# Layer boundary of a two-layer decoder trunk: a residual ahead of the next weights' splits, and norm weights applied per K tile

## The chip, the cores and the metric

The kernel runs on one core of a Trainium2 chip. The metric is the device time of one execution in microseconds (us); smaller is better. The engines of the core work in parallel, each through its own list of instructions in order: PE (matrix products and transposes), ACT (activations, copies), DVE (vector work), POOL (vector work as well) and SP, which here only issues the transfers from memory. An instruction starts when the one ahead of it on its engine has gone and the semaphores that it waits for are set.

## The reference

Two layers over 256 positions of width 1024, each x ← x + RMSNorm_post(mixer(RMSNorm_pre(x))). Layer 0 mixes with gated linear attention, layer 1 with compressed, selected and sliding-window attention. What matters here is the step from one layer to the next:

```
def rms_norm(x, g):
    xf = x.astype(jnp.float32)
    y = xf * lax.rsqrt(jnp.mean(xf * xf, axis=-1, keepdims=True) + NORM_EPS)
    return (y * g.astype(jnp.float32)).astype(x.dtype)
...
    for i in range(DEPTH):
        h = rms_norm(x, pre_norm[i])
        ...
            y = gla_mixer(h, ..., gla_w_out[j])      # ends in o @ w_out
        ...
            y = nsa_mixer(h, positions, nsa_w_in[j], ...)   # begins with h @ w_in
        x = x + rms_norm(y.astype(x.dtype), post_norm[i])
```

## The kernel before

The 256 positions are two tiles of 128 rows (t = 0, 1). The width of 1024 is 8 K tiles of 128, k0 to k7. To keep float32 accuracy in the faster product format, each operand is split into a rounded half, hi, and a remainder, lo = value − hi; a product of one K tile is then three matmuls, hi·hi, lo·hi and hi·lo (`mm3`). ACT writes every hi, DVE or POOL every lo.

**Weights** come in chunks of up to 512 columns. A chunk is 4 loads of two K tiles each into `raw` buffers, and 8 splits (`split_unit`): ACT copies a K tile of `raw` to `hi`, and DVE or POOL (by the table `LOS`) subtracts. Around the boundary these are `ch_o` (layer 0's output weights), `ch_kc` and `ch_ks` (the first two chunks of layer 1's input weights) and `ch_kw` after them.

**The boundary** is the loop over t that begins with `out_proj` (line 775). `out_proj(t)` multiplies layer 0's result with `ch_o` into two PSUM banks of 512 columns and calls `residual`: for each half, ACT squares the bank and sums the squares, DVE scales the bank by the norm weights into `yg`; after the second half POOL takes the power −0.5 of the sum, and DVE adds both halves to `X`. `pre_T(t, c)` then transposes `X[:, t]` on PE, four K tiles into one PSUM bank (c = 0: k0 to k3, c = 1: k4 to k7), applies layer 1's pre-norm weights (`gT`, one per row of the transpose) and splits the result into `hT`, the operand of every product of layer 1. `rms(t)` computes tile t's own factor, which is applied later.

Behind the boundary PE computes `kc_part(0)` and `ks_part(0)` (24 matmuls each, of tile 0 with `ch_kc` and `ch_ks`), then `kc_part(1)`, `ks_part(1)`, and then the products with `ch_kw`. In this text kc(0) is the 24 matmuls of `kc_part(0)`, and so on. They take k0 to k7 in turn. Small transposes stand between them: that of `vecs` (line 846; its copy on DVE is line 847) and the 16 of line 853.

The order on each engine is made when the program is built: a scheduler places the instructions by its own estimate of the time, within the order of the code and the extra edges of `after(...)`. Before, one such edge holds the first split of `ch_ks` behind the last hi of tile 0's `hT` (`ks_after`). The line numbers below are those of the kernel before; in the kernel after they differ by up to two.

Of the kernel before, what the change touches and what calls it, by code (L numbers as in the profile page):

```python
# [9 lines left out]
F32 = mybir.dt.float32  # L10
F32R = mybir.dt.float32r
I32 = mybir.dt.int32
AF = mybir.ActivationFunctionType
ALU = mybir.AluOpType
AX = mybir.AxisListType

P = 128
# [3 lines left out]
KT = D // P  # L21
# [66 lines left out]
def hybrid_kernel(ctx: ExitStack, tc: tile.TileContext, x, positions, pre_norm, post_norm,  # L88
# [3 lines left out]
    nc = tc.nc  # L92
    base = ctx.enter_context(tc.tile_pool(name="base", bufs=1))
# [4 lines left out]
    def nm(s):  # L98
        _n[0] += 1
        return f"{s}_{_n[0]}"  # L100

    def bank(tag="t"):
        return ps.tile([P, 512], F32, tag=tag, name=nm(tag), bufs=BANKS[tag])

    def f(ap):
        return ap.bitcast(F32)

    def after(ins, prev):

        if prev is not None:  # L110
            tc.add_manual_dep(ins.ins, prev.ins.name, mybir.DependencyInfo(
                mybir.DependencyClass.NoSync, mybir.DependencyReason.DATA), reason="issue order")
        return ins
# [103 lines left out]
    def chain(first, final):  # L217

        after(first, last[0])
        last[0] = final  # L220

    def proj(chunk, hT, t, tag="acc"):

        o = bank(tag)
        for k in range(KT):
            a, b = mm3(o[:, :chunk.n], [h[:, k, t * P:(t + 1) * P] for h in hT], chunk.part(k), k == 0, k == KT - 1)
            first = a if k == 0 else first
            chunk.mm[t * KT + k] = a
        chain(first, b)
        return o  # L230
# [24 lines left out]
    def rstd_of(ss, n, m, by=1.0):  # L255
# [4 lines left out]
        nc.gpsimd.tensor_tensor(r[:, :m], v[:, :m], half[:, :m], op=ALU.pow)  # L260
        return r

    def residual(t, o, gb):

        ss = base.tile([P, 8], F32, tag="ss", name=nm("ss"), bufs=4)
        yg = [base.tile([P, H], F32, tag="xg", name=nm("yg"), bufs=2) for _ in range(2)]

        def done(n):
            nc.scalar.activation(yg[n], o[n], AF.Square, accum_out=ss[:, n:n + 1])  # L269
            if n == 0:  # L270
                nc.vector.tensor_scalar(ss[:, 2:3], ss[:, 0:1], D * EPS, None, op0=ALU.add)
            else:

                nc.vector.tensor_add(ss[:, 4:5], ss[:, 1:2], ss[:, 2:3])
                nc.gpsimd.tensor_tensor(ss[:, 3:4], ss[:, 4:5], half[:, :1], op=ALU.pow)
            nc.vector.scalar_tensor_tensor(yg[n], o[n], float(D ** 0.5), gb[:, n * H:(n + 1) * H], op0=ALU.mult,  # L276
                                           op1=ALU.mult)
            if n == 1:
                for m in range(2):
                    xx = X[:, t, m * H:(m + 1) * H]  # L280
                    nc.vector.scalar_tensor_tensor(xx, yg[m], ss[:, 3:4], xx, op0=ALU.mult, op1=ALU.add)
        return done
# [8 lines left out]
    def new_hT():  # L291
        return [base.tile([P, KT, S], F32R, tag=f"hT{n}", name=nm("hT")) for n in "hl"]
# [2 lines left out]
        nc.scalar.activation(hi, bv, AF.Copy)  # L295
        nc.vector.tensor_sub(lo, bv, f(hi))

    def pre_T(t, c, layer, hT, tag, prev=None):

        b = bank(tag)  # L300
        for k in range(4):
            m = nc.tensor.transpose(b[:, k * P:(k + 1) * P], X[:, t, (c * 4 + k) * P:(c * 4 + k + 1) * P], ident)
            if layer == t == 0:
                chain(m, m)
        xg = base.tile([P, 4, P], F32, tag="xg", name=nm("xg"), bufs=2)
        g = gT[:, layer * KT + c * 4:layer * KT + c * 4 + 4]
        nc.vector.tensor_tensor(xg, b.rearrange("p (k n) -> p k n", k=4), g.unsqueeze(2).to_broadcast([P, 4, P]),
                                op=ALU.mult)
        hi, lo = (a[:, c * 4:c * 4 + 4, t * P:(t + 1) * P] for a in hT)
        m = after(nc.scalar.activation(hi, xg, AF.Copy), prev)  # L310
        nc.vector.tensor_sub(lo, xg, f(hi))  # L311
        return m

    onesr = base.tile([P, P], F32R, tag="onesr", name="onesr")
# [3 lines left out]
    def rms(t, prev=None):  # L318

        ss = base.tile([P, 8], F32, tag="ss", name=nm("ss"), bufs=4)  # L320
        for n in range(2):
            jk = base.tile([P, H], F32, tag="of", name=nm("junk"))
            m = after(nc.scalar.activation(jk, X[:, t, n * H:(n + 1) * H], AF.Square, accum_out=ss[:, n:n + 1]), prev)
        nc.vector.tensor_add(ss[:, 2:3], ss[:, 0:1], ss[:, 1:2])
        rs = rstd_of(ss[:, 2:3], D, 1)
        return rs[:, 0:1], m
# [13 lines left out]
    def out_proj(t, chunks, oT, gb):  # L340

        o = [bank("s"), bank("acc" if t else "s")]
        steps = [(k, n) for k in range(4) for n in range(2)] + [(k, n) for n in range(2) for k in range(4, KT)]
        done = residual(t, o, gb)
        for k, n in steps:
            a, b = mm3(o[n], [h[:, k, :] for h in oT[t]], chunks[n].part(k), k == 0, k == KT - 1)
            first = a if k == n == 0 else first
            if k == KT - 1:
                done(n)
        chain(first, b)  # L350
# [42 lines left out]
    hT = new_hT()  # L393
# [92 lines left out]
    gT = base.tile([P, 2 * KT], F32, tag="gT", name="gT")  # L486
# [75 lines left out]
    w, n = wraw[:RANK + 1], RANK + 1  # L562
# [24 lines left out]
    b = bank()  # L587
# [42 lines left out]
    scale = float(np.float32(GDK ** -0.5))  # L630
    aTs, qees, kdds = [], [], []
    for t in range(NT):
# [3 lines left out]
        for hp in range(2):  # L636
            b = bank()
# [4 lines left out]
            bv = b.rearrange("p (h n) -> p h n", h=2)  # L642
            nc.scalar.activation(E[:, 2 * hp:2 * hp + 2, :w], bv[:, :, :w], AF.Exp)
            last_exp = nc.scalar.activation(En[:, 2 * hp:2 * hp + 2, :], bv[:, :, :P], AF.Exp, scale=-1.0)
        if t == 0:
            b = bank()
# [9 lines left out]
        bv = qT[:, :, t * P:(t + 1) * P]  # L656
        nc.vector.scalar_tensor_tensor(qe, bv, scale, E[:, :, :P], op0=ALU.mult, op1=ALU.mult)
        if t == 1:
# [3 lines left out]
                                           op0=ALU.mult, op1=ALU.mult)  # L662
            qee = halves(qee, ("qeeh", "qeel"))
        b = bank()
        for h in range(GH):
            nc.tensor.transpose(b[:, h * P:(h + 1) * P], ksb[:, t, h * P:(h + 1) * P], ident)
        bv = b.rearrange("p (h n) -> p h n", h=GH)
# [26 lines left out]
    for t in range(NT):  # L694
        aT = aTs[t]
        ob = []
        for hp in range(2):
            b = bank("s")
            for hh in range(2):
                h = 2 * hp + hh  # L700
                o = b[:, hh * 256:(hh + 1) * 256]
# [4 lines left out]
        if t == 0:  # L706
            Ssb = [lp.tile([P, GH, GDV], F32R, tag=a, name=nm("S")) for a in ("q", "k")]
            for hp in range(2):
                b = bank("s")
# [8 lines left out]
        for h in range(GH):  # L718
            nc.vector.scalar_tensor_tensor(on[:, h * 256:(h + 1) * 256], ov[h], rs[:, h:h + 1], hn,
                                           op0=ALU.mult, op1=ALU.mult)  # L720
# [6 lines left out]
    for c in range(2):  # L727
# [4 lines left out]
        for t in range(NT):  # L732
            b = bank()
# [36 lines left out]
    hT = new_hT()  # L770
# [3 lines left out]
    for t in range(NT):  # L774
        out_proj(t, ch_o, oT, gpost)
        for c in range(2):
            last_hi = pre_T(t, c, 1, hT, "t")
        if t == 0:
            ks_after = last_hi
        rs1.append(rms(t)[0])  # L780
        for tab in (CSt, SNt):
            nc.vector.tensor_scalar(tab[:, t], tab[:, t], rs1[t], None, op0=ALU.mult)
# [3 lines left out]
    lp = ctx.enter_context(tc.tile_pool(name="l2", bufs=1))  # L786
    ch_kc.split()
    ch_ks = Chunk(w_in, N_KS, 512).load()
    ch_ks.split_unit(ks_after)
    ch_ks.split()  # L790
    vs_sb = lp.tile([P, NT, 256], F32, tag="vs", name="vs_sb")
    vw_sb = lp.tile([P, NT, 256], F32, tag="vw", name="vw_sb")
# [119 lines left out]
    for t in range(NT):  # L912
        o = proj(ch_kw[0], hT, t)
# [4 lines left out]
    for t in range(NT):  # L918
        o = proj(ch_kw[1], hT, t)
        nc.scalar.activation(vw_sb[:, t, 24:], o[:, :232], AF.Copy, scale=rs1[t])  # L920

        g = gates[:, t].rearrange("p h b -> p (h b)")
# [226 lines left out]
    def out_steps(t, before=None):  # L1149

        o = [bank("acc") for _ in range(2)]
        steps = [(k, n) for k in range(6) for n in range(2)] + [(k, n) for n in range(2) for k in range(6, KT)]
        done = residual(t, o, gpost)
        for k, n in steps:
            a, b = mm3(o[n], [h[:, k, :] for h in ofT[t]], ch_o[n].part(k), k == 0, k == KT - 1)
            if before and (k, n) == (LATE, 0):
                after(a, before())
            chain(a, b)
            if k == KT - 1:
                done(n)  # L1160
            yield 1
        for n in range(2):
            sl = slice(n * H, n * H + H)
            dma(out[0, t * P:(t + 1) * P, sl], X[:, t, sl])
# [7 lines left out]
    b = bank()  # L1172
# [8 lines left out]
    b = bank()  # L1181
# [84 lines left out]
```

## Time and profile before

| | before |
|---|---|
| median of 3 runs (lowest, highest) | 298.65 us (298.47, 299.83) |
| the profiled execution | 298.99 us, of which the traced span is 297.1 us |
| PE busy | 283.8 us, 96% of the span |
| DVE, ACT, POOL busy | 213.8, 178.7, 163.8 us |
| mean granted clock of PE | 0.995 |

PE is busy nearly throughout, so the time follows the few places at which it waits. The 1.9 us between the span and the time of the execution lie outside the trace. Times in rows are counted from the start of the span.

### The profile page before, as it was taken

The page shows a single profiled execution, that of the slowest core. Times are in us where ns is not written, and L with a number is a line of the kernel's source. Part 1 is how long each engine was busy: PE and PEld are TensorE (multiplying, and loading weights), DVE is VectorE, ACT ScalarE, POOL GpSimd, SP SyncE. Part 2 cuts the span into 40 slices and gives each one's busy share as a digit, 9 for nine tenths or more (in the row PEclk, how much of TensorE's full clock was granted, in tenths as well). Part 3 has the DMA queues.
Part 4 walks back from the last instruction along what each step waited for, and adds up shares of the span by engine and source line. Part 5 has one row for each costly group of instructions (what it writes and reads, how often), then busy time and mean ns, then how long its engine had stood idle before and what let it go on. Part 6 is the DMA issues. An engine that isn't in the chain of part 4 may idle for free.

```text
span 297.1 us, 5455 instructions
## 1 busy us (share of the span) xinstructions
PE 283.8 (96%) x1836; PEld 238.2 (80%) x1836; DVE 213.8 (72%) x552; ACT 178.7 (60%) x464; POOL 163.8 (55%) x184
## 2 busy tenths in 40 slices
PE   8999999999999999889999999999999979999991
PEld 7788999999999887668897789976887657677560
DVE  1679668854989968577459578799569988686423
ACT  3896788676665665444436526494568896475311
POOL 1396968985376132824539295479596545333200
PEclk9999999999999999999999999999999999999997
DMA  7996488114667244189896575607162000010001
GB/s 205 399 398 207 145 253 273 48 67 146 210 207 221 76 139 141 29 227 348 263 381 185 149 216 165 183 12 225 49 200 86 1 0 2 0 72 2 0 0 71
DMA packets 28300, 44.56 MB, mean 150 GB/s; under 512 B 2865, under 2 KB 12513, under 8 KB 28274
## 3 DMA queue, kind: packets, MB, share of 16 engines
q1 hardware_dynamic: 28242, 44.23, 47.2%
q8 instruction: 14, 0.23, 0.3%
q14 instruction: 12, 0.10, 0.1%
q10 hardware_dynamic: 32, 0.01, 0.0%
HBM read 43.18 MB, written 1.05 MB: 149 GB/s over the span
## 4 chain that ended last, share of the span: by engine, by line
PE 71%; DVE 11%; issue 8%; POOL 4%; ACT 2%; DMA 2%; SPq 0%; POOLq 0%; DVEq 0%; ACTq 0%
PE acc L213 12%; PE acc L211 12%; PE acc L212 12%; PE s L211 4%; PE s L212 4%; PE s L213 4%; PE s L468 4%; PE o L1105 3%; PE t L1091 3%; PE s L1018 3%; PE o L904 2%; DVE lo L196 2%; DVE P L1023 2%; DMA raw<-in_gla_w_in_dram 2%; PE o L1129 1%
## 5 line engine op out<-in xcount | busy, mean ns | idle before, releaser
L196 POOL TENSOR_TENSOR lo<-raw,hi 128x512 fp32r<-128x512 f32 (+2 forms) x63 | 83.6, 1349 | 42.1 <-ACT hi L190 41.1
L190 ACT ACTIVATE hi<-raw 128x512 fp32r<-128x512 f32 (+2 forms) x120 | 62.7, 582 | 17.8 <-DMA raw<-in_nsa_w_in_dram 6.2
L196 DVE TENSOR_TENSOR lo<-raw,hi 128x512 fp32r<-128x512 f32 (+2 forms) x57 | 54.5, 978 | 8.8 <-ACT hi L190 8.6
L1062 POOL TENSOR_SCALAR P<-P,cf 128x128 f32<-128x128 f32 (+1 forms) x64 | 28.0, 456 | 31.9 <-DVE cf L1058 9.1
L211 PE MATMUL acc<-hT,hi 128*128 128x256 f32 x160 | 45.0, 282 | 0.0
L212 PE MATMUL acc<-hT,hi 128*128 128x256 f32 x160 | 44.9, 281 | 0.0
L213 PE MATMUL acc<-hT,lo 128*128 128x256 f32 x160 | 44.5, 281 | 0.0
L1025 ACT ACTIVATE P<-P,mn 128x128 f32<-128x128 f32 (+1 forms) x64 | 28.4, 446 | 14.4 <-DVE mn L1023 10.4
L213 PE MATMUL acc<-hi,hT 128*128 128x512 f32 (+2 forms) x104 | 35.9, 346 | 0.8 <-DVE hT L311 0.8
L211 PE MATMUL acc<-hi,hT 128*128 128x512 f32 (+2 forms) x104 | 35.8, 345 | 0.8 <-DVE yg L276 0.8
L212 PE MATMUL acc<-lo,hT 128*128 128x512 f32 (+2 forms) x104 | 35.4, 341 | 0.0
L212 PEld LDWEIGHTS acc<-hT,hi 128*128 128x128 f32 x160 | 30.1, 188 | 0.3
L211 PEld LDWEIGHTS acc<-hT,hi 128*128 128x128 f32 x160 | 30.1, 188 | 0.1
L213 PEld LDWEIGHTS acc<-hT,lo 128*128 128x128 f32 x160 | 29.8, 188 | 0.0
L1023 DVE CUSTOM_DVE_ANT_0 P<-s,c 128x128 f32<-128x128 f32 (+1 forms) x64 | 20.9, 349 | 6.2 <-PE s L1018 4.8
L211 PEld LDWEIGHTS acc<-hi,hT 128*128 128x128 f32 x104 | 19.6, 188 | 3.7 <-ACT yg L269 1.2
L213 PEld LDWEIGHTS acc<-hi,hT 128*128 128x128 f32 x104 | 19.6, 188 | 3.4 <-DVE hT L311 1.7
L212 PEld LDWEIGHTS acc<-lo,hT 128*128 128x128 f32 x104 | 19.6, 188 | 1.7
L1091 PE MATMUL t<-c,P 128*128 128x128 f32 x96 | 18.3, 286 | 0.3 <-POOL P L1062 0.3
L440 POOL TENSOR_TENSOR lo<-raw,hi 128x512 fp32r<-128x512 f32 (+1 forms) x9 | 12.3, 1390 | 10.2 <-ACT hi L436 10.1
L1018 PE MATMUL s<-kTh,qS 128*128 128x272 f32 (+1 forms) x48 | 15.2, 329 | 2.2 <-DVE mn L1023 1.6
L1091 PEld LDWEIGHTS t<-c,P 128*128 128x128 f32 x96 | 10.9, 140 | 6.7 <-issue 3.5
(270 smaller groups left out, 673.8 us busy)
## 6 DMA issues: line engine op xcount, KB each, us to landing
raw<-in_nsa_w_in_dram SPq DMA_DIRECT2D x24, 512.0 KB, 4.3
raw<-in_gla_w_in_dram SPq DMA_DIRECT2D x12, 512.0 KB, 5.3
raw<-in_gla_w_out_dram SPq DMA_DIRECT2D x8, 512.0 KB, 4.3
raw<-in_nsa_w_out_dram SPq DMA_DIRECT2D x8, 512.0 KB, 4.1
raw<-in_nsa_w_in_dram SPq DMA_DIRECT2D x8, 280.0 KB, 6.1
raw<-in_gla_w_in_dram SPq DMA_DIRECT2D x6, 344.0 KB, 3.1
home<-in_gla_w_in_dram SPq DMA_DIRECT2D x4, 512.0 KB, 6.8
w<-in_nsa_ck_w_dram SPq DMA_DIRECT2D x4, 512.0 KB, 7.4
```

The lines of the kernel that those rows point to most:

```text
L190: m = after(nc.scalar.activation(hi[:, j, :n], raw[:, j, :n], AF.Copy), prev)
L196: eng.tensor_sub(lo[:, j, :n], raw[:, j, :n], f(hi[:, j, :n]))
L211: m = nc.tensor.matmul(o, a[0], b[0], start=start, stop=False, **kw)
L212: nc.tensor.matmul(o, a[0], b[1], start=False, stop=False, **kw)
L213: return m, nc.tensor.matmul(o, a[1], b[0], start=False, stop=stop, **kw)
L440: line(e, eng.tensor_sub(lo[:, j, :n], raw[:, j, :n], f(hi[:, j, :n])))
L468: m = nc.tensor.matmul(o[t][:, :chunk.n], hT[i][:, k, t * P:(t + 1) * P], w[j], start=(k == b == 0), stop=(k == KT - 1 and b == 2))
L1018: pe(nc.tensor.matmul(o, q[i], k[:, g, c0:c1], start=(m == 0), stop=(m == 1)))
L1023: nc.vector.tensor_tensor_reduce(out=o, in0=src, in1=masks[br], op0=ALU.add, op1=ALU.min, scale=-0.125, scalar=3.0e38, accum_out=self.mn[: ...
L1025: nc.scalar.activation(o, o, AF.Exp, scale=-1.0, bias=self.mn[:, j:j + 1], accum_out=self.sm[:, j:j + 1])
L1062: nc.gpsimd.tensor_scalar(o, o, cf[:, i * 2 + br:i * 2 + br + 1], 1.0, op0=ALU.mult, op1=ALU.mult)
L1091: pe(nc.tensor.transpose(b[:, i * P:(i + 1) * P], self.Pt[i][:, c0:c0 + P], ident))
```

## The change

Three edits. In `pre_T` the product with the norm weights, the copy to hi and the subtraction, each over four K tiles at once and through a buffer `xg`, become one pair per K tile straight from the PSUM bank: ACT copies with the weight as its scale, DVE multiplies and subtracts in one instruction. The buffer `xg`, which the residual's `yg` shares, is no longer used there. The edge on the first split of `ch_ks` now starts at the last square of tile 1's residual instead of at tile 0's hi.

```
-    def pre_T(t, c, layer, hT, tag, prev=None):
+    def pre_T(t, c, layer, hT, tag):
...
-        xg = base.tile([P, 4, P], F32, tag="xg", name=nm("xg"), bufs=2)
-        g = gT[:, layer * KT + c * 4:layer * KT + c * 4 + 4]
-        nc.vector.tensor_tensor(xg, b.rearrange("p (k n) -> p k n", k=4), g.unsqueeze(2).to_broadcast([P, 4, P]),
-                                op=ALU.mult)
-        hi, lo = (a[:, c * 4:c * 4 + 4, t * P:(t + 1) * P] for a in hT)
-        m = after(nc.scalar.activation(hi, xg, AF.Copy), prev)
-        nc.vector.tensor_sub(lo, xg, f(hi))
+        for k in range(4):
+            i = c * 4 + k
+            hi, lo = (a[:, i, t * P:(t + 1) * P] for a in hT)
+            bv, g = b[:, k * P:(k + 1) * P], gT[:, layer * KT + i:layer * KT + i + 1]
+            m = nc.scalar.activation(hi, bv, AF.Copy, scale=g)
+            nc.vector.scalar_tensor_tensor(lo, bv, g, f(hi), op0=ALU.mult, op1=ALU.subtract)
         return m
...
-            nc.scalar.activation(yg[n], o[n], AF.Square, accum_out=ss[:, n:n + 1])
+            squared[0] = nc.scalar.activation(yg[n], o[n], AF.Square, accum_out=ss[:, n:n + 1])
...
-            last_hi = pre_T(t, c, 1, hT, "t")
-        if t == 0:
-            ks_after = last_hi
+            pre_T(t, c, 1, hT, "t")
...
-    ch_ks.split_unit(ks_after)
+    ch_ks.split_unit(squared[0])
```

What this makes of the order. On ACT at the boundary, from the last square of `rms(0)` on, the order before was (`xg_237` and `xg_239` hold k0 to k3 and k4 to k7 of tile 0; `hi_271` to `hi_277` are the four pairs of `ch_ks`; `yg_248` and `yg_249` the two squares of tile 1's residual):

```order
L323 ACTIVATE junk_242_1410,ss_240_1407<-x_sb_73 128x512
L310 ACTIVATE hT_225_1317<-xg_237_1394 128x4x128
L310 ACTIVATE hT_225_1317<-xg_239_1403 128x4x128
L190 ACTIVATE hi_271_1547<-raw_267_1539 128x512 x2
L190 ACTIVATE hi_273_1553<-raw_268_1541 128x512 x2
L190 ACTIVATE hi_275_1559<-raw_269_1543 128x512 x2
L190 ACTIVATE hi_277_1565<-raw_270_1545 128x512 x2
L269 ACTIVATE yg_248_1422,ss_247_1421<-s_245_1419 128x512
L269 ACTIVATE yg_249_1423,ss_247_1421<-acc_246_1420 128x512
```

Now it is as follows, from the second square on (bank `t_236` holds k0 to k3 of tile 0, `t_237` k4 to k7; the square of the first half, three pieces of `t_236`, k0 to k2, and two of `t_237`, k4 and k5, stand ahead of these rows; `hi_267` to `hi_273` are the pairs of `ch_ks`):

```order
L271 ACTIVATE yg_247_1431,ss_245_1429<-acc_244_1428 128x512
L190 ACTIVATE hi_267_1563<-raw_263_1555 128x512 x2
L190 ACTIVATE hi_269_1569<-raw_264_1557 128x512 x2
L190 ACTIVATE hi_271_1575<-raw_265_1559 128x512
L311 ACTIVATE hT_225_1317<-t_237_1402,gT_126 128x128
L190 ACTIVATE hi_271_1575<-raw_265_1559 128x512
L190 ACTIVATE hi_273_1581<-raw_266_1561 128x512 x2
L311 ACTIVATE hT_225_1317<-t_236_1389,gT_126 128x128
```

The squares moved ahead of the eight splits; the fourth piece of `t_236`, which is k3 of tile 0, now stands behind all eight of them, and the third of `t_237`, k6, among them.

On DVE the order now is, from the third piece of `t_236` (k2) on (`lo_268` and `lo_270` are the DVE's four splits of `ch_ks`; before, they stood behind all of tile 0's `hT` and ahead of the residual):

```order
L312 SCALAR_TENSOR_TENSOR hT_226_1318<-t_236_1389,gT_126,hT_225_1317 128x128
L276 TENSOR_TENSOR ss_245_1429<-ss_245_1429 128x1
L278 SCALAR_TENSOR_TENSOR yg_247_1431<-acc_244_1428,gpost_148_858 128x512
L196 TENSOR_TENSOR lo_268_1564<-raw_263_1555,hi_267_1563 128x512
L283 SCALAR_TENSOR_TENSOR x_sb_73<-yg_246_1430,ss_245_1429,x_sb_73 128x512
L283 SCALAR_TENSOR_TENSOR x_sb_73<-yg_247_1431,ss_245_1429,x_sb_73 128x512
L196 TENSOR_TENSOR lo_268_1564<-raw_263_1555,hi_267_1563 128x512
L196 TENSOR_TENSOR lo_270_1570<-raw_264_1557,hi_269_1569 128x512 x2
L312 SCALAR_TENSOR_TENSOR hT_226_1318<-t_237_1402,gT_126,hT_225_1317 128x128
L847 COPY vT_1610<-o_279_1638 128x32
L312 SCALAR_TENSOR_TENSOR hT_226_1318<-t_236_1389,gT_126,hT_225_1317 128x128
```

The residual of tile 1 moved ahead of three of the four splits, and the lo of k3 (the last row) stands behind all of them and behind the copy of `vecs`.

On PE the rows of kc(0) that use k3 now are these (`acc_277` is its bank; `t_248` is the first bank of tile 1's transposes):

```order
L213 MATMUL acc_277_1611<-hi_257_1537,hT_226_1318 128x512
L846 MATMUL o_279_1638<-c0_64,vecs_1597 128x32
L211 MATMUL acc_277_1611<-hi_257_1537,hT_225_1317 128x512
L212 MATMUL acc_277_1611<-lo_258_1538,hT_225_1317 128x512
L304 MATMUL t_248_1489<-c0_64,x_sb_73 128x128 x4
L213 MATMUL acc_277_1611<-hi_257_1537,hT_226_1318 128x512
```

The transpose of `vecs` and tile 1's transposes moved into kc(0); before, they stood behind ks(0). The other four transposes of tile 1 now stand ahead of the last matmul of kc(0), and the 16 of line 853 behind the sixth matmul of kc(1).

## Rows read from the trace of the kernel before

**Rows 1.** Windows: busy us and count per engine, PE's granted clock, DMA.

```profile
115.90:144.50 28.60, 26.46 (x143) 20.32 (x143) 18.54 (x42) 13.87 (x33) 13.30 (x15) 1.00 0.65 194
144.50:290.90 146.40, 143.57 (x949) 112.71 (x947) 108.92 (x363) 84.60 (x250) 78.96 (x101) 1.00 0.34 106
```

**Rows 2.** Chain that ended last, at the boundary: start, us, engine and line.

```profile
124.73 0.52 POOL ss L275
125.27 1.32 DVE x_sb L281
...
131.84 1.32 DVE hT L311
```

**Rows 3.** Timeline of PE: start, us, line, tiles; in brackets idle and releaser.

```profile
113.66 1.03 PE L302 MATMUL t<-c,x_sb 128*128 128x128 f32 x8
...
115.69 0.40 PE L213 MATMUL acc<-hi,oT 128*128 128x512 f32 x1
116.16 0.50 PE L211 MATMUL acc<-hi,hT 128*128 128x512 f32 x1
...
121.88 0.40 PE L213 MATMUL acc<-hi,hT 128*128 128x512 f32 x1
123.04 0.47 PE L211 MATMUL acc<-hi,hT 128*128 128x512 f32 x1 [0.76 <-DVE yg L276]
...
130.56 0.69 PE L853 MATMUL t<-c,rt 128*64 128x64 f32 x16 [0.49 <-DVE vT L847]
...
131.65 0.50 PE L211 MATMUL acc<-hi,hT 128*128 128x512 f32 x1
...
133.21 0.50 PE L213 MATMUL acc<-hi,hT 128*128 128x512 f32 x1 [0.83 <-DVE hT L311]
...
144.49 0.29 PE L211 MATMUL acc<-hi,hT 128*128 128x280 f32 x1
```

**Rows 4.** Timeline of ACT at the boundary.

```profile
116.61 4.26 ACT L190 ACTIVATE hi<-raw 128x512 fp32r<-128x512 f32 x8
120.77 0.57 ACT L269 ACTIVATE yg<-s 128x512 f32<-128x512 f32 x1
```

**Rows 5.** Timeline of DVE at the boundary.

```profile
110.00 3.49 DVE L196 TENSOR_TENSOR lo<-raw,hi 128x512 fp32r<-128x512 f32 x2
...
114.75 1.28 DVE L307 TENSOR_TENSOR xg<-t,gT 128x512 f32<-128x512 f32 x2
...
117.35 2.49 DVE L196 TENSOR_TENSOR lo<-raw,hi 128x512 fp32r<-128x512 f32 x4
...
122.21 0.68 DVE L276 SCALAR_TENSOR_TENSOR yg<-acc,gpost 128x512 f32<-128x512 f32 x1
```

**Rows 6.** Timeline of POOL at the boundary.

```profile
109.65 3.29 POOL L196 TENSOR_TENSOR lo<-raw,hi 128x512 fp32r<-128x512 f32 x2 [1.02 <-ACT hi L190]
...
119.43 5.29 POOL L196 TENSOR_TENSOR lo<-raw,hi 128x512 fp32r<-128x512 f32 x4 [5.05 <-ACT hi L190]
```

**Rows 7.** Instructions of lines 419 and 424 (layer 0's pieces): ns min/median/max.

```profile
L419 ACT ACTIVATE hT<-t,gT x8: 348/366/378, 5.3 to 8.2; 128x128 fp32r<-128x128 f32 x8
...
L424 DVE SCALAR_TENSOR_TENSOR hT<-t,gT,hT x8: 341/343/351, 6.5 to 9.4; 128x128 fp32r<-128x128 f32 x8
```

**Rows 8.** Instructions that write vecs: SP's issue, and the landing of its transfers.

```profile
L125 SPq DMA_DIRECT2D vecs<-in_nsa_pe_v_dram x1: 418/418/418, 124.9 to 124.9; - x1
...
DMA to landing us min/median/max: 1.7/1.7/1.8
```

**Rows 9.** Timeline of SP: the first transfer behind the boundary.

```profile
122.96 0.88 SPq L125 DMA_DIRECT2D w<-in_nsa_ck_w_dram  x2
```

**Rows 10.** Windows at the end of the span, columns as in rows 1.

```profile
290.50:291.00 0.50, 0.41 (x2) 0.00 (x0) 0.50 (x1) 0.05 (x1) 0.00 (x0) 1.00 0.00 0
...
293.50:294.00 0.50, 0.00 (x0) 0.00 (x0) 0.41 (x1) 0.00 (x0) 0.00 (x0) 1.00 0.00 0
294.00:294.50 0.50, 0.00 (x0) 0.00 (x0) 0.00 (x0) 0.00 (x0) 0.00 (x0) 0.61 0.77 303
```

More of the change, by code (lines that the diff above doesn't have):

```diff
@@ L261, in rstd_of @@
         return r
+    squared = [None]
     def residual(t, o, gb):
```

## The prediction

> **What bounds the kernel now.** The windows on either side of the moment at which PE begins `ch_kw` come first [rows 1]. From 144.5 to 290.9 us PE is busy for 143.57 of 146.40 us: behind the boundary it has 2.83 us of slack in all, so whatever the boundary gains or loses arrives at the end nearly whole. From 115.9 to 144.5 it is idle for 2.14 us, and the change can win only there. PE's timeline names the places [rows 3]: out_proj(1) ends at 115.92 (its last matmul starts at 115.69, and 20 of kc(0)'s gaps up to 121.88 are 0.233 us each), kc(0) begins at 116.16; ks(0) begins at 123.04, where the row says 0.76 idle, because its bank is freed only when DVE has scaled tile 1's residual; line 853 waits 0.49 for the copy of `vecs`; kc(1) begins at 131.65 and waits 0.83 for tile 1's `hT`. The chain of waits gives the reason: between 124.73 and 133.2 it runs off PE, through the power, the update of `X` and the last subtraction into `hT` of tile 1 [rows 2]. That chain starts late because the two squares of the residual (120.77 and 0.57 later) stand behind eight splits that ACT began at 116.61 [rows 4]. So the slot is real, and the waits that the change could remove sum to 0.24 + 0.76 + 0.49 + 0.83 = 2.3 us.
>
> **The change, part by part.** *The squares ahead of the splits.* ACT and DVE do the same residual work, some 4 us earlier. It frees the bank of ks(0) before PE wants it, and starts tile 1's update of `X` sooner. The transfers of layer 1's small tensors move along: the first one waited for the scaling by `gpost`, which ended at 122.21 + 0.68 = 122.89 against the issue at 122.96 [rows 5, 9].
>
> *The pieces per K tile.* Removed for each tile are two products into `xg`, two copies and two subtractions over 512 columns. Added are eight ACT pieces of 0.37 us and eight DVE pieces of 0.34 us, priced by layer 0's same instructions [rows 7]. For two tiles that makes 5.9 us of ACT and 5.5 us of DVE. For tile 1 they lie beside ks(0) and kc(1) on PE, which need nothing from them until kc(1) begins, and I cost them at nothing; without that cover each pair of one bank would cost 0.7 us, since hi and lo of a bank alternate in the built order. For tile 0 they stand on the path: PE takes k0 to k7 in turn and needs hi and lo of each.
>
> *What is late now.* The built order puts the hi of k3 behind all eight splits of `ch_ks` on ACT, and its lo behind three splits on DVE. ACT, DVE and POOL take their lists in order, so this is a wait that no early finish elsewhere can lift. I walk it through.
>
> ACT: the eight transposes of tile 0 begin at 113.66 and take 1.03 [rows 3], so the first bank is there at about 114.2 and hi of k0 at 114.55. DVE comes free where its first `xg` stood, at 114.75 [rows 5]; it now scales the first half first (0.68), so lo of k0 ends at 115.85. Hi and lo alternate with the other bank's pieces in between: hi of k2 ends at 116.95, its lo at 117.3. Then the second square (0.57) to 117.5; eight splits at 0.52 (116.61 to 120.77 for eight [rows 4]) and the piece of k6 among them (0.37) to 122.05; hi of k3 at 122.4.
>
> DVE: the sum of squares is there at 117.6; scaling (0.68), one split (0.62, as 2.49 for four [rows 5]), two updates of `X` (1.32 in the chain [rows 2]) take it to 120.35. Then three splits, and POOL begins its own four at 120.3, when ACT has written their hi. That price is the open one. With POOL idle a DVE split takes 0.62; beside two POOL splits (109.65, 3.29 for two) two DVE splits took 3.49, 1.75 each [rows 5, 6]. The bounds are 0.62 and 1.75; I take 1.75, since here too POOL runs splits without a break from before the first of the three to after the last, 5.29 for four [rows 6]. The three end at 125.65, the piece of k6 and the copy of `vecs` (0.3 together) follow, and lo of k3 ends at 126.3.
>
> The Trainium skill bears on this price: "SBUF — State Buffer", section "Who interferes with whom", says that a DVE instruction with two SBUF inputs and a GpSimd instruction that reads SBUF exclude each other, and that the second to issue waits for the whole of the first. By it each of the three would wait out one POOL split of about 1.3 and then run its own 0.62, some 1.9 instead of 1.75, and the sum below would be 0.5 us more. The page also frees instructions with one SBUF input from this, which would leave the pieces themselves at 0.34.
>
> PE, against that: out_proj(1) ends at 115.92; kc(0) starts there, 0.24 earlier than before, and k0 to k2 are nine matmuls, to 118.02. Then the transpose of `vecs`: its transfers begin when DVE has scaled the second half, at 118.4 instead of 122.89; the last one was issued 1.95 later and landed 1.7 after that [rows 8, 9], so 122.1, and PE stands until then. Next hi of k3: two matmuls from 122.45 to 122.9. Then tile 1's first transposes wait for the bank that lo of k3 frees, and the third matmul of k3 for that lo itself: 126.4. So PE waits 4.4 us and then 3.5 us. From there on nothing waits: four transposes 0.5 (half of 1.03), twelve matmuls 2.8, four transposes 0.5, one matmul 0.2: 130.4. ks(0), 24 matmuls, 5.6: 136.0. kc(1): six matmuls, line 853 (130.56 to 131.65, 1.1), 18 matmuls: 142.7. ks(1) with four transposes of `dup`, 6.1: 148.8. There `ch_kw` begins, which before was 144.49 [rows 3]. Its loads start some 3 us earlier than before, so they don't hold it.
>
> **Sum:** 148.8 − 144.5 = 4.3 us later. As a check, the new waits are 7.9 us; the old ones, 2.3, go, and tile 1's transposes and `vecs`, which then stood alone between two projections, now overlap waits or matmuls. On the profiled execution this makes 298.99 + 4.3 = 303.3 us; the median of the runs shown is 0.34 lower than that execution, so 303.0 us.
>
> **The rivals.** *PE's clock falls in the new waits.* At the end of the span PE's last matmul ended at 290.91, and the granted clock was still 1.00 in the half microsecond up to 294.0 and fell to half (2.4 to 1.2 GHz) in the next one: some 3.2 us without work were enough [rows 10]. The two new waits, 4.4 and 3.5 us, are longer than that, with only two matmuls and one small transpose between them. Against it: those three are work. If the clock falls, matmuls from 126.4 on run at half speed until it returns. No row shows how long that takes; a stretch as long as the fall took (3.2 us) would cost 1.6 us, twice that 3.2: 304.6 to 306.2 us. The Trainium skill, "TensorE: Matmul & The Clock Gate", section "What's actually happening", says that an idle engine is gated to 1.2 GHz and that sustained work brings 2.4 GHz back; the tail agrees with its first half, and no row here shows its second.
>
> *DVE isn't slowed.* If the three splits take 0.62 each, DVE is through at 122.3, lo of k3 follows its hi at 122.9, and the second wait (3.5) is gone: +0.8, 299.5 us. For it speaks that DVE's four at 117.35 took 2.49, against it that POOL was idle then until 119.43 [rows 5, 6].
>
> *The delay is given back later.* All of PE's slack behind the boundary is 2.83 us [rows 1]. Were all of it waits for supplies that now come in time, +1.5 would be left: 300.1 us. Against it: the loads and splits behind the boundary follow the buffers that PE, DVE and POOL free, and so move with them.
>
> *Faster.* The old waits go (2.3, and about 1.3 that transposes and `vecs` cost alone) and PE doesn't stand at k3: 4.3 − 7.9 = −3.6, 295.0 us. It needs hi of k3 when PE has done k2. The point from which it decides is a total of 3.6 us for the new waits: with the second one gone, hi of k3 would have to come by 121.6, 0.8 earlier than worked out, which means eight splits at 0.42. The eight of before ran at 0.52 without a gap [rows 4].
>
> **How the numbers follow.** Waits at k3 with the clock at full: 0.50. The same and the clock falls: 0.28. DVE not slowed: 0.10. Given back: 0.05. Faster: 0.07. The likeliest is 303.0 us. The range reaches from 299.8 to 305.6: below it are the faster case and more than half of the unslowed one (0.13), above it the long half-clock stretch (0.06). A measurement of this kernel can tell about 0.5%, 1.5 us, from no change: 297.15 to 300.15. Faster is its own case, 0.07; the unslowed case and part of the given-back one fall within, 0.13; the rest is slower, 0.80.
>
> **What would show it.** After kc(0)'s ninth matmul PE idles some 4 us, released by ACT's `hT`, and again some 3 us at the transposes of tile 1 or the third matmul of k3, released by DVE's `hT`. The waits at ks(0) and kc(1) are gone. ACT shows the second square at about 117 and the fourth piece of its bank at about 122, behind eight splits. `ch_kw` begins near 149. If the granted clock shows a window under 1.00 near 125 to 130, the first rival holds. The prediction is wrong if PE goes through k3 without a wait, or if the first wait is there and the kernel is no slower; then slack behind the boundary was larger than rows 1 say. It is wrong in size if DVE's three splits take less than 1.2 us each.

## The result, and the profile after

The changed kernel takes 303.13 us (median of four executions, 301.23 to 304.85) against 299.0 of before in the same session: ratio 1.0134, interval [1.0103, 1.0164]. Run again beside the experiments it took 302.01 us (six executions, 301.7 to 302.7): 1.0106, [1.0076, 1.0136]. So it is slower, by 3 to 4 us.

The first profile was taken of the slowest of the four executions (304.85 us), and 1.9 us of that were there before the change begins: tile 0's eight transposes stand at 115.53 in it, at 113.66 in [rows 3] and at 113.80 in the profile taken beside the experiments. That offset belongs to the execution and is taken off below by reading differences: from the first matmul of kc(0) to the first of `ch_kw` it was 144.49 − 116.16 = 28.3 us before [rows 3], or 28.6 from the end of out_proj(1), and is 149.70 − 117.80 = 31.9 after (PE goes from out_proj(1) into kc(0) without a gap now).

PE's timeline after, from the ninth matmul of kc(0) on and then the first of `ch_kw`, answers to [rows 3]; the brackets give idle time and what is held to have ended it:

```profile
119.66 0.40 PE L213 MATMUL acc<-hi,hT 128*128 128x512 f32 x1
124.28 0.28 PE L846 MATMUL o<-c,vecs 32*128 32x32 f32 x1 [4.22 <-DVE hT L312]
124.49 0.80 PE L211 MATMUL acc<-hi,hT 128*128 128x512 f32 x1
125.09 0.63 PE L212 MATMUL acc<-lo,hT 128*128 128x512 f32 x1
125.51 1.05 PE L304 MATMUL t<-c,x_sb 128*128 128x128 f32 x4
126.22 0.78 PE L213 MATMUL acc<-hi,hT 128*128 128x512 f32 x1
126.79 0.63 PE L211 MATMUL acc<-hi,hT 128*128 128x512 f32 x1
...
128.93 0.59 PE L213 MATMUL acc<-hi,hT 128*128 128x512 f32 x1
129.35 0.39 PE L211 MATMUL acc<-hi,hT 128*128 128x512 f32 x1
...
149.70 0.29 PE L211 MATMUL acc<-hi,hT 128*128 128x280 f32 x1
```

Three things are to be seen. The ninth matmul's successor could have started at 119.66 + 0.23 = 119.89 and started at 124.28: one wait of 4.4 us. There is no second one at line 304 or at k3's third matmul (126.22). And the matmuls behind the wait stand 0.43 apart (126.79 to 128.93) and not 0.23, until 129.35. The waits of before at ks(0), line 853 and kc(1) are gone.

ACT's timeline has the order that was forecast, the eight splits and k6 ahead of k3's piece, which ends at 124.06; it answers to [rows 4]:

```profile
118.72 0.59 ACT L271 ACTIVATE yg<-acc 128x512 f32<-128x512 f32 x1
...
119.29 2.70 ACT L190 ACTIVATE hi<-raw 128x512 fp32r<-128x512 f32 x5
121.89 0.36 ACT L311 ACTIVATE hT<-t,gT 128x128 fp32r<-128x128 f32 x1
122.14 1.67 ACT L190 ACTIVATE hi<-raw 128x512 fp32r<-128x512 f32 x3
123.70 0.36 ACT L311 ACTIVATE hT<-t,gT 128x128 fp32r<-128x128 f32 x1
```

DVE's answers to [rows 5]. The two updates of `X` at 120.71 take 0.70 each and the three splits at 122.03 take 1.88 together, 0.63 each:

```profile
120.71 1.40 DVE L283 SCALAR_TENSOR_TENSOR x_sb<-yg,ss,x_sb 128x512 f32<-128x512 f32 x2
122.03 1.88 DVE L196 TENSOR_TENSOR lo<-raw,hi 128x512 fp32r<-128x512 f32 x3
123.84 0.34 DVE L312 SCALAR_TENSOR_TENSOR hT<-t,gT,hT 128x128 fp32r<-128x128 f32 x1
124.60 0.19 DVE L847 COPY vT<-o 128x32 f32<-128x32 f32 x1 [0.42 <-PE o L846]
124.71 0.60 DVE L312 SCALAR_TENSOR_TENSOR hT<-t,gT,hT 128x128 fp32r<-128x128 f32 x2
```

POOL's four splits in the same stretch (ns: shortest, median, longest; begin of the first and of the last) answer to [rows 6]: it is POOL whose first split took 2.93 us, while DVE's three ran; the others took 1.27.

```profile
L196 POOL TENSOR_TENSOR lo<-raw,hi x4: 1267/1277/2927, 122.1 to 127.5; 128x512 fp32r<-128x512 f32 x4
```

SP's timeline has the transfers behind the boundary 2.7 us earlier than [rows 9], 4.6 with the offset taken off; those of `vecs` are issued at 121.70 and 122.21:

```profile
120.27 0.88 SPq L125 DMA_DIRECT2D w<-in_nsa_ck_w_dram  x2
...
121.70 0.47 SPq L125 DMA_DIRECT2D vecs<-in_nsa_pe_k_dram  x1
122.21 0.42 SPq L125 DMA_DIRECT2D vecs<-in_nsa_pe_v_dram  x1
```

With the landing time of [rows 8], 1.7, the second of them lands at 123.9. The transpose of `vecs` at 124.28 waits for it, and k3's hi was there at 124.06: two suppliers end the one wait within 0.2 us. The bracket names DVE's `hT`, which line 846 doesn't read; in an execution of another kernel below the same wait is put down to the transfer. In all six profiles here in which line 846 stands behind a wait, whatever its bracket names, it starts 0.3 to 0.5 us after its last transfer landed.

The windows, with the columns of [rows 1], show the granted clock (third number from the right). It is 1.00 up to some 122.5, 2.4 us after PE's last matmul ended at 120.06, then 0.50 (1.2 GHz), and full again from some 129.3:

```profile
121.00:122.00 1.00, 0.00 (x0) 0.00 (x0) 1.00 (x2) 1.00 (x3) 0.00 (x0) 1.00 0.37 86
122.00:123.00 1.00, 0.00 (x0) 0.00 (x0) 1.00 (x3) 1.00 (x3) 0.88 (x1) 0.75 0.54 117
...
128.00:129.00 1.00, 1.00 (x4) 0.73 (x3) 0.35 (x1) 0.58 (x2) 1.00 (x2) 0.50 0.95 246
129.00:130.00 1.00, 1.00 (x5) 0.82 (x4) 0.70 (x4) 0.26 (x2) 0.27 (x1) 0.83 0.97 334
```

From 124.49 to 129.35 PE did nine matmuls and four transposes; at full clock they are 9 × 0.233 + 0.5 = 2.6 us, so the low clock cost 2.3 us here.

### The profile page after: what moved, and what is told of

It reads as the page before. It is cut to its first block, busy times and chain, and to the rows that moved or that the text cites. A ratio compares the mean times of both kernels' runs of the same rounds, so it can differ in the third digit from the quotient of the medians.

```text
span 303.1 us, 5472 instructions
## 1 busy us (share of the span) xinstructions
PE 287.5 (95%) x1836; PEld 242.0 (80%) x1836; DVE 214.4 (71%) x560; ACT 181.8 (60%) x476; POOL 166.1 (55%) x184
## 4 chain that ended last, share of the span: by engine, by line
PE 70%; DVE 12%; issue 8%; DMA 4%; POOL 3%; ACT 1%; SPq 0%; POOLq 0%; DVEq 0%; ACTq 0%
PE acc L211 12%; PE acc L213 12%; PE acc L212 12%; PE s L211 4%; PE s L212 4%; PE s L213 4%; PE s L469 4%; DVE lo L196 3%; PE o L1105 3%; PE t L1091 3%; PE s L1018 3%; DMA raw<-in_nsa_w_in_dram 3%; PE o L904 2%; DMA raw<-in_gla_w_in_dram 2%; DVE P L1023 2%
## 5 line engine op out<-in xcount | busy, mean ns | idle before, releaser
L196 POOL TENSOR_TENSOR lo<-raw,hi 128x512 fp32r<-128x512 f32 (+2 forms) x63 | 85.9, 1384 | 38.0 <-ACT hi L190 35.7
L196 DVE TENSOR_TENSOR lo<-raw,hi 128x512 fp32r<-128x512 f32 (+2 forms) x57 | 53.1, 951 | 7.4 <-ACT hi L190 7.2
L1062 POOL TENSOR_SCALAR P<-P,cf 128x128 f32<-128x128 f32 (+1 forms) x64 | 28.1, 460 | 31.9 <-DVE cf L1058 9.0
L213 PE MATMUL acc<-hi,hT 128*128 128x512 f32 (+2 forms) x104 | 36.7, 353 | 0.0
L211 PE MATMUL acc<-hi,hT 128*128 128x512 f32 (+2 forms) x104 | 36.6, 352 | 0.0
L212 PE MATMUL acc<-lo,hT 128*128 128x512 f32 (+2 forms) x104 | 36.1, 347 | 0.0
L211 PEld LDWEIGHTS acc<-hi,hT 128*128 128x128 f32 x104 | 20.1, 193 | 2.3 <-ACT hi L190 0.4
L213 PEld LDWEIGHTS acc<-hi,hT 128*128 128x128 f32 x104 | 20.0, 192 | 1.8
```

The source lines that it names most:

```text
L196: eng.tensor_sub(lo[:, j, :n], raw[:, j, :n], f(hi[:, j, :n]))
L211: m = nc.tensor.matmul(o, a[0], b[0], start=start, stop=False, **kw)
L212: nc.tensor.matmul(o, a[0], b[1], start=False, stop=False, **kw)
L213: return m, nc.tensor.matmul(o, a[1], b[0], start=False, stop=stop, **kw)
L1062: nc.gpsimd.tensor_scalar(o, o, cf[:, i * 2 + br:i * 2 + br + 1], 1.0, op0=ALU.mult, op1=ALU.mult)
```

## The experiments

The seven kernels ran in two sessions, e1 to e4 and e5 to e7, in which before had medians of 298.78 and 298.82 us. "Boundary" is the time from the first matmul of kc(0) to the first of `ch_kw`, and "low clock" the stretch at 0.50 worked out from rows of 1 us.

| kernel | median us | ratio to before [interval] | boundary us | low clock |
|---|---|---|---|---|
| before | 298.8 | | 28.3 | none |
| changed, first profile | 303.13 | 1.0134 [1.0103, 1.0164] | 31.9 | 122.5 to 129.3 |
| e5_again: changed | 302.01 | 1.0106 [1.0076, 1.0136] | 31.2 | 122.4 to 125.8 |
| e1_pieces_first | 296.46 | 0.9909 [0.9888, 0.9930] | 25.9 | none |
| e2_vecs_first | 302.03 | 1.0099 [1.0071, 1.0127] | 30.8 | 121.9 to 125.4 |
| e3_vecs_kept | 300.81 | 1.0060 [1.0039, 1.0080] | 30.5 | 121.9 to 125.3 |
| e4_filler | 300.98 | 1.0063 [1.0044, 1.0082] | 29.6 | none |
| e6_squares_only | 297.04 | 0.9939 [0.9921, 0.9957] | 26.3 | none |
| e7_pool_first | 306.69 | 1.0260 [1.0228, 1.0292] | 35.7 | 121.3 to 131.6 |

**Is it the pieces, or their place?** Against the changed kernel, only what the first split waits for is put back:

```diff
-            pre_T(t, c, 1, hT, "t")
+            last_hi = pre_T(t, c, 1, hT, "t")
+        if t == 0:
+            ks_after = last_hi
...
-    ch_ks.split_unit(squared[0])
+    ch_ks.split_unit(ks_after)
```

> The changed kernel, but the first split of the next weights waits on ACT for the last piece of tile 0 (as in the kernel before) and not for the last square, so that all eight pieces of tile 0 stand ahead of the eight splits; the transpose of vecs then stands behind four matmuls of ks(0). Theory (the loss is the place of k3's pieces and of the transpose of vecs, not the pieces): PE doesn't stand in kc(0), the granted clock stays at 1.00 there, the squares are still ahead of the splits. From the end of out_proj(1) to the begin of ch_kw 5.6 + 1.0 + 0.1 + 5.6 + 6.7 + 6.1 = 25.1 us against 28.6 before and 31.9 after: 295.5 us, 295 to 297. Rival A (the pieces themselves cost, 16 more instructions on ACT and 16 longer ones on DVE): the wait moves to the first matmuls of ks(0) or to kc(1), 299 us or more. Rival B (the gain is given back behind the boundary): ch_kw begins 3 us early and the end is at 298 to 299.

PE's timeline of it: kc(0) begins at 116.45, tile 1's eight transposes run at 122.31, and no row between them and `ch_kw` at 142.31 has a wait:

```profile
116.45 0.39 PE L211 MATMUL acc<-hi,hT 128*128 128x512 f32 x1
...
122.31 1.04 PE L304 MATMUL t<-c,x_sb 128*128 128x128 f32 x8
...
142.31 0.29 PE L211 MATMUL acc<-hi,hT 128*128 128x280 f32 x1
```

The place was the loss. With all pieces of tile 0 ahead of the splits the clock stays up and the boundary takes 25.9 us; the 25.1 worked out ahead was 0.8 short. Most of that, 0.5 us, still lies at k3, though no bracket marks it: its three matmuls and the one behind them start 0.30 to 0.46 apart (118.31 to 119.74) and not 0.23. The kernel is 2.3 us faster than before (0.9% by the ratio), and both rivals are out.

**k3's hi, or `vecs`?** Two kernels take one of the two suppliers away. In the first, `vecs` comes early:

```diff
+    dma(vecs[0:16, :], nsa_pe_k[0].rearrange("(j t) d -> j (t d)", t=2))
+    dma(vecs[16:32, :], nsa_pe_v[0].rearrange("(j t) d -> j (t d)", t=2))
     for i, src in enumerate((nsa_ck_w2, nsa_ck_w2, nsa_cv_w2)):
         dma(w2[:, :, i], src[0].rearrange("(a p) n -> p a n", p=P))
-    dma(vecs[0:16, :], nsa_pe_k[0].rearrange("(j t) d -> j (t d)", t=2))
-    dma(vecs[16:32, :], nsa_pe_v[0].rearrange("(j t) d -> j (t d)", t=2))
```

> The changed kernel with one edit: the two transfers of vecs are issued ahead of the three of w2, so that they land about 1.5 us earlier. In the trace of the changed kernel the first wait ended at 124.28 where vecs had landed, and hi of k3 was written at 124.06, so either would have held PE. Theory: the wait then stands at the first matmul of k3, ends with ACT's piece some 0.2 us earlier than after, the clock falls as it did, and the time is that of the changed kernel less 0.2: 302.9 us (301 to 304). Rival (vecs was the cause of the wait and hi of k3 only beside it): the wait shrinks by about 1.5 us and the time falls by 1.5 to 3: 300 to 301.5 us.

PE's timeline (kc(0) begins at 115.77):

```profile
120.56 0.21 PE L846 MATMUL o<-c,vecs 32*128 32x32 f32 x1 [2.52 <-DVE x_sb L283]
122.09 0.80 PE L211 MATMUL acc<-hi,hT 128*128 128x512 f32 x1 [1.32 <-ACT hT L311]
```

The transpose of `vecs` now stands in the middle of the wait, and PE goes on waiting for ACT. From the begin of kc(0) k3 starts 122.09 − 115.77 = 6.3 us later; in the changed kernel it was 124.49 − 117.80 = 6.7. The time is that of the changed kernel in the other session (302.03 and 302.01). The rival, which had the wait 1.5 us shorter, is out.

In the second, k3's hi is early, as in e1_pieces_first, and the transpose of `vecs` is pinned to where the changed kernel has it. Against e1_pieces_first (`at3` is called in `proj` ahead of k3, for tile 0 of kc alone):

```diff
+            if at3 is not None and k == 3:
+                chain(first, b)
+                first = None
+                at3()
...
+        def at3():
+            vb.append(bank("o"))
+            m = nc.tensor.transpose(vb[0][:, :32], vecs, ident[:32, :32])
+            chain(m, m)
...
-            b = bank("o")
-            nc.tensor.transpose(b[:, :32], vecs, ident[:32, :32])
-            nc.vector.tensor_copy(vT, b[:, :32])
+            nc.vector.tensor_copy(vT, vb[0][:, :32])
```

> As e1_pieces_first, but the transpose of vecs is pinned behind k2 of kc(0), where the changed kernel has it, so vecs alone can hold PE there; the eight transposes of tile 1 stand ahead of it and fill a part of the wait. Theory (vecs lands about 4.1 us after k2 is done, whatever ACT does): PE still waits there, some 3.1 us beside the 1.0 of transposes, and the boundary takes 28 us: 298.5 us with the clock at full, up to 300.5 where it falls. Rival (hi of k3 was the only cause): no wait, as e1_pieces_first, about 295.5 us.

The waits in kc(0) and the first matmul of k3, in its PE timeline:

```profile
118.83 0.66 PE L308 MATMUL t<-c,x_sb 128*128 128x128 f32 x4 [1.36 <-DVE x_sb L287]
119.76 0.66 PE L308 MATMUL t<-c,x_sb 128*128 128x128 f32 x4 [0.27 <-DVE hT L316]
121.90 0.28 PE L849 MATMUL o<-c,vecs 32*128 32x32 f32 x1 [1.48 <-DMA vecs<-in_nsa_pe_v_dram]
122.11 0.80 PE L211 MATMUL acc<-hi,hT 128*128 128x512 f32 x1
```

They are 1.36 + 0.27 + 1.48 = 3.1 us, as expected; the clock falls too, and the time is 0.3 above the upper end given for that, at 300.81. The boundary is 4.6 us longer than in e1_pieces_first, from which only the place of that transpose differs (tile 1's transposes moved with it). With the transposes in the wait, k3 starts 122.11 − 115.21 = 6.9 us after the begin of kc(0). So each of the two suppliers alone holds k3 about as long as both together (6.3 and 6.9 against 6.7), and both had to go.

**What does the clock cost?** Against the changed kernel, with the same `at3` in `proj`:

```diff
+        def at3():
+            wb = bank("o")
+            for _ in range(16):
+                m = nc.tensor.matmul(wb, hT[0][:, 0, :P], ch_kc.part(0)[0], start=True, stop=True)
+                chain(m, m)
```

> The changed kernel with 16 more matmuls of 128x512 behind k2 of kc(0), into the bank that vecs uses next; their results are not used. They take 16 x 0.233 = 3.7 us, less than the first wait of 4.4, so nothing is later by them. Theory (the fall of the granted clock is the second half of the loss): the clock stays at 1.00 from 120 to 132, the first wait shows 0.5 to 0.9 us in place of 4.4, matmuls behind it stand 0.233 apart, ch_kw begins 2.3 us earlier against out_proj(1)'s end than in the changed kernel (29.5 in place of 31.9 us), and the time falls by about 2 us to 301 us, with less spread between executions. Rival A (the low clock is not what cost the time, PE would have waited for lo parts of POOL and DVE there anyway): matmuls at full clock, but new waits, time as after, 303. Rival B (the fall comes from elsewhere than the idle time): the clock falls all the same, 303 us.

PE's timeline behind the 16 matmuls:

```profile
122.08 0.21 PE L856 MATMUL o<-c,vecs 32*128 32x32 f32 x1 [0.51 <-DVE hT L316]
```

The windows in which the clock falls without them:

```profile
121.00:122.00 1.00, 0.57 (x3) 0.13 (x1) 1.00 (x4) 1.00 (x4) 1.00 (x1) 1.00 0.42 50
122.00:123.00 1.00, 0.92 (x5) 0.78 (x6) 0.67 (x3) 1.00 (x4) 1.00 (x2) 1.00 0.76 197
```

The wait left is 0.5 us, the clock stays at 1.00, and the boundary is 29.6 us (29.5 expected), 1.5 to 2.3 less than in the two profiles of the changed kernel. So work that is thrown away makes the kernel faster, 300.98 against 302.01 us in the other session, with intervals that overlap by a little. Rivals A and B are out at the boundary. Whether the spread between executions shrinks isn't settled: the twelve here span 2.5 us, the changed kernel's 3.6 (four) and 1.0 (six). Of the gain a part is lost behind it: from `ch_kw` to the end of PE's last matmul it took 147.6 us here, 146.4 before, and one wait stands out there (total, times, longest), which the kernel before does not show:

```profile
PE t L841 <- POOL dup L834: 1.0, 1, 1.0
```

**Does the boundary repeat?** The changed kernel again:

> The changed kernel unchanged, on the same chip as the next two. Theory: the two waits and the fall of the clock are the program's own, so the boundary (first matmul of kc(0) to first of ch_kw) again takes 30.8 to 31.9 us and the time is 302.5 us (301 to 304); the offset of 1.9 us ahead of the boundary in the first profile is not. Rival (the offset belongs to the change): tile 0's transposes start at 115.5 again.

Tile 0's transposes and the wait, in PE's timeline:

```profile
113.80 1.03 PE L304 MATMUL t<-c,x_sb 128*128 128x128 f32 x8
...
122.65 0.28 PE L846 MATMUL o<-c,vecs 32*128 32x32 f32 x1 [4.32 <-DVE hT L312]
```

The windows in which the clock falls and comes back:

```profile
122.00:123.00 1.00, 0.35 (x2) 0.32 (x2) 0.48 (x3) 1.00 (x5) 1.00 (x1) 0.70 0.78 213
...
125.00:126.00 1.00, 1.00 (x4) 0.76 (x4) 1.00 (x3) 0.34 (x1) 1.00 (x2) 0.59 0.88 164
126.00:127.00 1.00, 1.00 (x6) 0.82 (x5) 0.54 (x2) 0.37 (x1) 1.00 (x1) 1.00 0.93 225
```

PE's timeline has the wait again (4.32) and no offset, and the windows have the low clock for half as long: back at full at about 125.8. Behind the wait its chain of waits has five matmuls and four transposes from 122.93 to 126.10, of which these are the first and the last:

```profile
122.93 0.72 PE acc L211
...
125.79 0.31 PE acc L212
```

They take 3.2 us where 5 × 0.233 + 0.5 = 1.7 would do: 1.5 us lost, not 2.3. That is the difference between the two profiles at the boundary (31.2 and 31.9 us).

**The squares alone.** Against the kernel before:

```diff
-            nc.scalar.activation(yg[n], o[n], AF.Square, accum_out=ss[:, n:n + 1])
+            squared[0] = nc.scalar.activation(yg[n], o[n], AF.Square, accum_out=ss[:, n:n + 1])
...
-    ch_ks.split_unit(ks_after)
+    ch_ks.split_unit(squared[0])
```

> The kernel before with one half of the change: the first split of the next weights waits on ACT for the last square; the weights of the norm are still applied for a whole bank through xg. In the built order both copies of tile 0 then stand ahead of the squares, and the squares ahead of the splits. Theory (the slot at the boundary is won by the squares' place alone): no wait in kc(0), ks(0) and kc(1), boundary 25.9 us as in e1_pieces_first, 296.5 us. Rival (the pieces bring a part: xg and the residual's scaled halves share two buffers, so without the pieces the residual waits for xg): the squares don't come earlier than the buffers, a wait of 1 to 2 us is left, 297.5 to 298.5 us.

ACT's timeline has both squares ahead of the splits, the first at 117.32 where [rows 4] have 120.77 (tile 0's transposes begin 0.4 later here):

```profile
117.32 0.60 ACT L271 ACTIVATE yg<-s 128x512 f32<-128x512 f32 x1 [0.22 <-DVE hT L313]
...
117.93 0.60 ACT L271 ACTIVATE yg<-acc 128x512 f32<-128x512 f32 x1
...
118.52 4.27 ACT L190 ACTIVATE hi<-raw 128x512 fp32r<-128x512 f32 x8
```

It takes 297.04 us, 1.8 us under before, with a boundary of 26.3 us, and lies between the theory (296.5) and the rival (297.5), nearer to neither. Its trace is nearer the theory: the waits of before at ks(0), line 853 and kc(1) are gone, and the buffer shared with `xg` holds the first square for 0.22 us, not for 1 to 2. The 0.24 us of before between out_proj(1) and kc(0), which the column leaves out, are still there (0.23). Of the 0.45 us by which its boundary is longer than that of e1_pieces_first, 0.37 is a wait of PE for a `dup` on POOL. Most of the slot is won by the place of the squares. The pieces may add half a microsecond (0.9909 against 0.9939, intervals that overlap), the 0.23 ahead of kc(0) among it; that isn't settled.

**Who waits, DVE or POOL?** One entry of the table, for `ch_ks`, against the changed kernel:

```diff
-(3, 5, 6), (4, 5, 6, 7), (1, 2, 4, 5, 7)
+(3, 5, 6), (0, 1, 2, 3), (1, 2, 4, 5, 7)
```

> The changed kernel with one number of the table changed: POOL takes the first four lo splits of ch_ks in place of the last four, so it starts while DVE is still at the residual; PE's order is unchanged. Theory (POOL runs and DVE waits when POOL is there first; in the changed kernel DVE's unbroken run was there first and POOL's first split took 2.9 us): the two updates of X take 1.4 to 1.9 each in place of 0.70, DVE's splits the same, lo of k3 comes 2 to 3 us later than its hi, and a second wait of that length appears at tile 1's first transposes: 304 to 306 us. Rival (DVE always goes first): updates and splits stay at 0.70 and 0.62, POOL's splits stretch, and the time is the changed kernel's.

Its timeline of DVE, from tile 1's updates of `X` on:

```profile
118.11 3.43 DVE L283 SCALAR_TENSOR_TENSOR x_sb<-yg,ss,x_sb 128x512 f32<-128x512 f32 x2
121.46 1.75 DVE L196 TENSOR_TENSOR lo<-raw,hi 128x512 fp32r<-128x512 f32 x1
...
123.39 2.10 DVE L196 TENSOR_TENSOR lo<-raw,hi 128x512 fp32r<-128x512 f32 x2
```

POOL's, with its four splits:

```profile
118.04 1.27 POOL L196 TENSOR_TENSOR lo<-raw,hi 128x512 fp32r<-128x512 f32 x1
...
119.35 4.99 POOL L196 TENSOR_TENSOR lo<-raw,hi 128x512 fp32r<-128x512 f32 x3
```

And PE's two waits:

```profile
122.21 0.28 PE L846 MATMUL o<-c,vecs 32*128 32x32 f32 x1 [4.29 <-DMA vecs<-in_nsa_pe_v_dram]
...
126.51 1.11 PE L304 MATMUL t<-c,x_sb 128*128 128x128 f32 x4 [2.86 <-DVE hT L312]
```

POOL starts at 118.04, DVE's update at 118.11, and now DVE pays: 1.72 an update, 1.75 the first split, 2.10 the next two together, during which POOL ends (124.34). Lo of k3 is late, and the second wait is there, 2.86 us at tile 1's first transposes. The rival is out. The time is 0.7 above the upper end of what was expected, because the clock is low for 10 us: from 122.42 to 131.64 PE did twelve matmuls and four transposes, 3.3 us at full clock, in 6.4 us beside the wait, so it lost 3.1 us and not the 1.5 of e5_again. The first wait's row here names the transfer of `vecs`.

## Why the prediction was right, and where it wasn't

It gave 303.0 us and 0.80 for slower; 303.13 and 302.01 were measured. The place and the sign were right, but of the two waits that made its size only one exists, and what two of the rivals held came in place of the other: DVE wasn't slowed (given 0.10) and the clock fell (given 0.28, beside both waits). The forecast had no case with both together. That 3.5 us fell away and 1.5 to 2.3 came in is why the time still came near 303.0, and that is luck.

*The slot and the old waits.* Right. The waits of before went, and the two kernels that have no long wait at k3 won 1.8 and 2.3 us; the rival on the other side, 3.6 us, was the right mechanism and too large. Its point of decision, hi of k3 by 121.6, left out `vecs`, which the same walk has at 122.1; with hi early and `vecs` as it was, PE still waited 3.1 us (e3_vecs_kept).

*The first wait.* Right: 4.4 us forecast, 4.4 and 4.5 measured from start to start (4.22 and 4.32 in the brackets), with `vecs` and k3's hi 0.3 us apart in the walk and 0.2 in the trace.

*The second wait.* This step failed: "I take 1.75, since here too POOL runs splits without a break from before the first of the three to after the last". The three splits took 0.63 each, under the 1.2 that the forecast itself named as the sign of a wrong size, and the 3.5 us of waiting didn't come. The price was right for its condition, which wasn't met: in the trace DVE was in a row of instructions with two SBUF inputs when POOL arrived, 0.09 us behind DVE's first split (122.12 against 122.03), and POOL waited out the rest of that row; e2_vecs_first, e5_again and e6_squares_only have the same (1.89 for DVE's three). With POOL there first one split took 1.75 and the wait appeared (e7_pool_first). The walk had the two starts 0.05 us apart, with POOL first, too near to choose by, and in it too DVE's second update, up to 120.35, was still running when POOL came at 120.3. The Trainium skill, "SBUF — State Buffer", section "Who interferes with whom", says "Issue order, not op shape, decides who blocks"; the two traces agree (2.93 us for POOL's first split in the one, 1.72 to 1.75 for DVE's instructions in the other); the forecast had reckoned DVE as the second.

*The rival on the clock.* It happened, and I had given it 0.28 beside the second wait, not in its place. Its price, 1.6 to 3.2 us, was about right: 1.5 and 2.3 us by the two profiles of the changed kernel. With both waits, as it was put, it stands in e7_pool_first: 3.1 us, and 306.69 against 304.6 to 306.2. What I held against it, that two matmuls and a transpose stand between the waits, had no part: the first wait was enough. The fall came 2.4 us after PE's last matmul in one profile and some 4.1 in the other, and not at the 3.2 of the span's end. The Trainium skill, "TensorE: Matmul & The Clock Gate", section "What's actually happening", says that sustained work brings 2.4 GHz back; the trace now shows that half too, at 129.3 and 125.8.

*The sum.* The walk went from 115.92 to 148.8, 32.9 us. Without the 3.5 of the second wait it is 29.4; the kernel with the filler, which has neither, shows 29.6. With the clock's 1.5 or 2.3 it is 30.9 or 31.7, and 31.2 and 31.9 were measured. So the boundary costs 2.6 to 3.3 us and not 4.3 (against 28.6 from the end of out_proj(1)), and the first median, 303.13, has a further piece of luck in it: from `ch_kw` to the end of PE's last matmul, where I forecast no difference, the first profile has another 0.7 us (before ends at 290.91):

```profile
296.45 0.40 PE L213 MATMUL acc<-hi,ofT 128*128 128x512 f32 x1
```

```profile
PE t L837 <- POOL dup L830: 0.5, 1, 0.5
```

That is 296.85 − 149.70 = 147.15 against 146.42. 0.5 of it is the wait of the second row, for a `dup` on POOL. Apart from e4_filler, the profiles of the other runs show no such wait behind `ch_kw`, the changed kernel's second among them, and lie between 0.1 us less and 0.3 us more than before; e6_squares_only has one of 0.37 ahead of it. What makes `dup` late in three of the executions was not tried, and stays open.

## What to carry to other kernels

When a step is moved ahead of a batch, look up in the built order what went behind the batch, and what now stands ahead of its own supply: here the gain was real, and one piece of 0.37 us behind eight splits and one transpose ahead of its transfer turned it into a loss. An idle stretch of PE is to be priced with what it does to the clock behind it, and two suppliers that arrive together must both be moved before anything is won. Whether DVE or POOL paid for their overlap went here by which one was in its run first, so a price read from one overlap needs the order of the two starts beside it.

## What the runs showed that was not expected

- POOL got no turn at all between DVE's instructions: its first split of 2.93 us from 122.12 is about what was left of DVE's three (1.88 from 122.03) and 1.27 of its own. In the other order both paid: 1.72 and 1.75 for DVE's instructions, 4.99 for three of POOL's splits, as if they took turns.
- Two waits of nearly the same length (4.2 and 4.3 us in the brackets) were followed by 6.8 us of low clock in one profile of the changed kernel and 3.4 in the other; and in e3_vecs_kept the clock fell although eight transposes, 1.3 us of work, stood in the wait. What decides how long the clock stays low was not tried.
